# A hybrid diffusion layer stack: the scan begins along the first gate, and scan and attention get smaller shares per weight block

## The chip, the cores and the metric

The kernel runs on one core of one Trainium2 chip. The time is the device time of one execution in microseconds (us). Engines are named as in the profile: PE is TensorE, DVE VectorE, ACT ScalarE, POOL GpSimd, SP SyncE. Each engine works through a queue of its own in a fixed order; an instruction that has to wait holds up everything behind it on its engine.

## The reference

The kernel computes two layers over 256 latent tokens and, in the first layer, 256 context tokens, with 1024 channels. Everything is in float32.

```python
h_l = modulate(rms_norm(x, norm_mix[layer]), mod_l[0], mod_l[1])
# token mixer: three branches on the same input
ssd_l  = ssd_output(y_lf, y_lb, xs_l, h_lat @ w_z, ...)         # two-way state-space scan, 16 heads of 64
na_l   = na_latent(h @ w_q, h @ w_k, h @ w_v, k_c, v_c, rpb) @ na_out   # softmax attention, 8 heads of 64
conf_l = conformer_branch(h @ w_glu, ...)                       # gated, 31-tap convolution per channel
out    = merge_branches(h @ w_gate, (ssd_l, na_l, conf_l)) @ w_o  # sum of sigmoid(gate_b) * branch_b
x = x + mod_l[2] * out
# feed-forward: SwiGLU in layer 0, the best two of eight SwiGLU experts in layer 1
x = x + mod_l[5] * f(modulate(rms_norm(x, norm_ffn[layer]), mod_l[3], mod_l[4]))
```

The scan takes `u`, a five-tap convolution of `h @ w_xbc`, in chunks of 128 tokens: states per chunk (`stS`), a diagonal part per chunk (`ydS`, a 128 x 128 matrix of decays times `C·B`, applied to the inputs), and a part from the carried state.

## The kernel before

All weight products are made in three matmuls of halves: a weight block of 128 x 1024 comes by DMA, ACT makes its high part `h_` (L114) and DVE the low part `l_` (L115), and PE forms high·high, high·low and low·high (L185 to L187). `wstat` keeps a block of weights still and moves the tokens; 512 output columns at a time, in four PSUM banks (the pool `pacc`), from four weight blocks. The next 512 columns can begin only when the four banks were evacuated; for a gate that is ACT's sigmoid at L643.

Token mixing in a layer is a row of steps, named in `ORDER`: `glu`, `dt`, `qkv`, `xbc` make the inputs of the branches, `g0` to `g2` the three gates, `z` the scan's output gate, `p0` to `p2` multiply the branch 0 (scan), 1 (attention), 2 (convolution) by its output weights. The step `ssd` multiplies nothing: it spawns the scan.

Beside these steps run background jobs, written as generators that emit a piece of work and yield its cost: `attention` (L679 ff.; scores S L705, softmax L709 to L714, scaling of P L693, its transposes PT L696, the copy of PT L698, products with v, `po`, L740), `ssd` (states L866 to L900, diagonal part L963 to L989 with the transposes `cbS` L981 and the mask product `MS` L986), `conformer` (31 taps, L534), and the modulation vectors. After each weight block `pump()` (L148) gives each job a credit, its number in `RATE` for this layer, and lets it emit pieces until the credit is spent. `branch` (`p0` to `p2`) first drains its job: all that is left of it is emitted at once. The credits thus set how far a job is spread along the weight blocks. A scheduler with the priorities of `PR` then puts the instructions of each engine into their fixed order.

Background work has four other PSUM banks (`pwk`). Layer 0 works on 512 tokens, layer 1 on 256, so a weight matmul is 128 x 512 there and 128 x 256 here. The profiled execution has the mixer of layer 0 from about 30 to 700 us, its feed-forward to 1150, the mixer of layer 1 to 1560, routing to 1590, and the experts to the end.

Of the kernel before, what the change touches and what calls it, by code (L numbers as in the profile page):

```python
# [53 lines left out]
class Body:  # L54
# [481 lines left out]
    def mix(self, l):  # L536
# [11 lines left out]
        def glu():  # L548
# [15 lines left out]
            cv = self.chunks(4, nt, f"ccv{l}")  # L564
            jobs[2] = self.spawn(self.conformer(l, cu, cv, nt), self.RATE["conv"][l], "conv")

        def qkv():
# [6 lines left out]
            r[1] = self.pair(4, nt, f"o{l}")  # L574
            jobs[1] = self.spawn(self.attention(l, q, kT, v, nt, r[1]), self.RATE["att"][l], "att")

# [5 lines left out]
        def ssd():  # L582
            jobs[0] = self.spawn(self.ssd(l, nt), self.RATE["ssd"][l], "ssd")

        def z():
            zs = self.chunks(KD, nt, "z" + nm)
            self.wstat(W("z"), KD, D, h, tok, lambda o, ps: nc.scalar.activation(zs[o], ps, AF.Silu), "z" + nm)
            if jobs[0] not in self.bg:
                jobs[0] = self.spawn(iter(()), self.RATE["ssd"][l], "ssd")
            jobs[0][0] = chain(jobs[0][0], self.ssd_norm(l, zs, nt))  # L590
# [10 lines left out]
        steps = dict(dt=lambda: self.dt_path(l), glu=glu, qkv=qkv, xbc=xbc, ssd=ssd, z=z)  # L601
        for s in self.ORDER[l].split():
            if s in steps:
# [5 lines left out]
            if full and s == "p1":  # L609
                jobs[3] = self.spawn(self.adas(0, (1, 2)), self.RATE["ada"][0], "ada")  # L610
            if s == "dt" and self.stop == "dt":
# [20 lines left out]
            self.route_ahead(*self.mc[1, 1])  # L632
        self.out_res(self.units(self.a["w_o"][l], 4), KD, m_, range(tok[0] // 128, NB), "wo" + nm)

    ORDER = ("glu dt qkv xbc g1 ssd p1 g2 p2 z g0 p0", "glu dt qkv xbc g1 ssd p1 g2 z p2 g0 p0")
    RATE = dict(conv=(2.0, 2.5), att=(5.0, 2.5), ssd=(7.0, 10.0), ada=(2.6, 2.2))

    def gate(self, l, br, tok):

# [932 lines left out]
    def run(self):  # L1572
# [3 lines left out]
        with ExitStack() as st:  # L1576
# [3 lines left out]
            for l in range(DEPTH):  # L1580
# [12 lines left out]
                if l == 0:  # L1593
                    with self.prio("norm"):
                        self.h = self.hmod(self.col("nffn"), *self.mc[0, 1], f"f{l}")
                    self.mrow = self.mod_rows(self.mod[0, 2], 2, f"f{l}", streams)
                    jobs = [self.spawn(self.adas(1, range(3)), self.RATE["ada"][1], "ada")]
                    self.ffn(0)
# [120 lines left out]
```

## Time and profile before

| what | value |
|---|---|
| three runs | 2400.76, 2401.92, 2401.93 us; median 2401.92 |
| the profiled execution | 2402.24 us, its span 2400.4 us |
| PE busy | 2284.4 us, 95% of the span |
| DVE busy | 1519.2 us, 63% |
| ACT busy | 1041.5 us, 43% |
| mean granted clock of PE | .984 of full speed |

The span reaches from the first to the last instruction; the time of the execution is 1.84 us longer. Busy shares are means over stages with different limits, so they say which engine to look at, and a table by stretch says where. PE's clock has two levels, 1.2 and 2.4 GHz; the granted clock of a stretch is the mean over it, 1.00 for 2.4 GHz.

### The profile page before, as it was taken

To read this page: it belongs to the slowest core of one execution; us is meant where nothing else is said; L and a number is where in the kernel's file an instruction comes from. 1 tells how busy PE (TensorE), PEld (TensorE's weight loads), DVE (VectorE), ACT (ScalarE), POOL (GpSimd) and SP (SyncE) were. 2 spreads that over 40 slices of the span, in tenths; PEclk is the share of its full clock that TensorE was granted. 3 is DMA by queue.
4 is the path that set the end of the run, shared out by engine and by line. 5 is a ranking of instruction groups with operands and counts; after the bars stand their busy time and mean duration, and the time that the engine had idled before them with its cause. 6 is when DMAs were issued, how large, how long until landed. Compare 5 with 4: busy or idle time off the path is not lost.

```text
span 2400.4 us, 30300 instructions
## 1 busy us (share of the span) xinstructions
PE 2284.4 (95%) x11409; PEld 1668.1 (69%) x11409; DVE 1519.2 (63%) x2389; ACT 1041.5 (43%) x1696; POOL 19.0 (1%) x32
## 2 busy tenths in 40 slices
PE   7999989999999999999999999989999998999997
PEld 3777757777777777788877889865666655656554
DVE  3669977677767775535889866643333545655556
ACT  4335645654233222224436585533332444445444
POOL 0000000000000000000000000000000000000000
PEclk9999999999999999999999999979999999999998
DMA  7222223234534555432422333468888899999995
GB/s 275 84 83 79 89 74 97 79 98 127 168 123 135 163 187 182 153 97 96 130 93 88 106 106 123 132 248 331 325 326 342 325 360 374 359 380 341 352 365 223
DMA packets 106283, 469.33 MB, mean 196 GB/s; under 512 B 11536, under 2 KB 12048, under 8 KB 72336
## 3 DMA queue, kind: packets, MB, share of 16 engines
q1 hardware_dynamic: 105280, 464.69, 53.9%
q10 hardware_dynamic: 848, 2.62, 0.3%
q8 instruction: 91, 1.49, 0.2%
q14 instruction: 64, 0.52, 0.1%
HBM read 466.22 MB, written 1.05 MB: 195 GB/s over the span
## 4 chain that ended last, share of the span: by engine, by line
PE 80%; DVE 9%; DMA 5%; ACT 3%; issue 2%; POOL 0%; SPq 0%; POOLq 0%; DVEq 0%; ACTq 0%
PE er L1470 8%; PE nn L1352 7%; PE e L1470 4%; PE edr L1470 4%; DMA adaw<-in_ada_w_dram 4%; PE ndn L1377 4%; PE wg L185 2%; PE wg L186 2%; PE wg L187 2%; PE ed L1470 2%; DVE adac L351 2%; PE xbcL L185 1%; PE ydS L989 1%; PE xbcL L187 1%; PE xbcL L186 1%
## 5 line engine op out<-in xcount | busy, mean ns | idle before, releaser
L351 DVE SCALAR_TENSOR_TENSOR adac<-adaw,sc,adac 128x512 f32<-128x512 f32 x224 | 160.6, 747 | 57.5 <-DMA adaw<-in_ada_w_dram 57.0
L115 DVE TENSOR_TENSOR l_er<-r_er,h_er 128x1024 fp32r<-128x1024 f32 x132 | 154.7, 1219 | 59.8 <-ACT h_er L114 57.6
L1352 PE MATMUL nn<-r_ngun,xn 128*64 128x512 f32 (+1 forms) x768 | 169.3, 561 | 0.0
L114 ACT ACTIVATE h_er<-r_er 128x1024 fp32r<-128x1024 f32 x132 | 133.4, 1053 | 41.7 <-DMA r_er<-in_moe_gu_dram 28.2
L185 PE MATMUL wg<-hHm,h_wg 128*128 128x512 f32 (+1 forms) x384 | 131.4, 343 | 0.0
L187 PE MATMUL wg<-hHm,l_wg 128*128 128x512 f32 (+1 forms) x384 | 130.6, 343 | 0.0
L186 PE MATMUL wg<-hLm,h_wg 128*128 128x512 f32 (+1 forms) x384 | 130.5, 341 | 0.0
L1470 PE MATMUL er<-h_er,gHp 128*128 128x512 f32 (+1 forms) x288 | 110.7, 389 | 17.7 <-ACT h_er L114 17.7
L1352 PEld LDWEIGHTS nn<-r_ngun,xn 128*64 128x64 f32 x768 | 54.3, 137 | 92.1 <-issue 85.1
L1470 PE MATMUL er<-h_er,gLp 128*128 128x512 f32 (+1 forms) x288 | 108.1, 380 | 0.0
L115 DVE TENSOR_TENSOR l_e<-r_e,h_e 128x1024 fp32r<-128x1024 f32 x44 | 52.3, 1222 | 63.2 <-ACT h_e L114 63.0
L1377 PE MATMUL ndn<-r_ndn,hnn 128*64 128x512 f32 x352 | 87.4, 598 | 0.0
L534 DVE SCALAR_TENSOR_TENSOR ccv<-cu,cols,ccv 128x492 f32<-128x492 f32 (+14 forms) x120 | 85.9, 729 | 1.0
L1357 ACT ACTIVATE ntn<-nn 128x512 f32<-128x512 f32 (+1 forms) x24 | 13.5, 561 | 165.7 <-PE nn L1352 165.7
L1470 PE MATMUL er<-l_er,gHp 128*128 128x512 f32 (+1 forms) x288 | 84.0, 380 | 0.0
L1367 DVE TENSOR_TENSOR hnn<-npn,nsn 128x256 f32<-128x256 f32 (+1 forms) x24 | 9.6, 401 | 117.3 <-ACT nsn L1365 117.3
L1470 PEld LDWEIGHTS er<-h_er,gHp 128*128 128x128 f32 x288 | 55.1, 191 | 40.2 <-ACT h_er L114 28.0
L115 DVE TENSOR_TENSOR l_edr<-r_edr,h_edr 128x1024 fp32r<-128x1024 f32 x66 | 77.5, 1220 | 5.8 <-ACT h_edr L114 4.5
L185 PEld LDWEIGHTS wg<-hHm,h_wg 128*128 128x128 f32 x384 | 73.1, 190 | 9.7 <-issue 2.2
L186 PEld LDWEIGHTS wg<-hLm,h_wg 128*128 128x128 f32 x384 | 73.1, 190 | 9.1 <-issue 2.0
L187 PEld LDWEIGHTS wg<-hHm,l_wg 128*128 128x128 f32 x384 | 72.7, 190 | 9.2 <-issue 1.7
L185 PE MATMUL xbcL<-hHm,h_xbcL 128*128 128x512 f32 (+1 forms) x192 | 74.9, 390 | 0.0
(656 smaller groups left out, 6067.5 us busy)
## 6 DMA issues: line engine op xcount, KB each, us to landing
r_ngun<-in_moe_gu_dram SPq DMA_DIRECT2D x88, 1024.0 KB, 7.1
r_er<-in_moe_gu_dram SPq DMA_DIRECT2D x66, 1024.0 KB, 7.3
r_ndn<-in_moe_down_dram SPq DMA_DIRECT2D x44, 1024.0 KB, 7.3
adaw<-in_ada_w_dram SPq DMA_DIRECT2D x160, 256.0 KB, 3.1
r_edr<-in_moe_down_dram SPq DMA_DIRECT2D x33, 1024.0 KB, 7.6
r_wg<-in_w_in_dram SPq DMA_DIRECT2D x48, 512.0 KB, 3.5
r_e<-in_moe_gu_dram SPq DMA_DIRECT2D x22, 1024.0 KB, 7.3
r_xbcL<-in_w_in_dram SPq DMA_DIRECT2D x24, 512.0 KB, 3.5
```

The costliest lines, as they stand in the source:

```text
L114: nc.scalar.activation(Hd, src, AF.Copy)
L115: nc.vector.tensor_tensor(Ld, src, Hd.bitcast(F32), op=ALU.subtract)
L185: mm(out, wh, xh, start=(first and kk == 0), stop=False, skip_group_check=True)
L186: mm(out, wh, xl, start=False, stop=False, skip_group_check=True)
L187: mm(out, wl, xh, start=False, stop=(kk == kc - 1), skip_group_check=True)
L351: nc.vector.scalar_tensor_tensor(d, w, c, d, op0=ALU.mult, op1=ALU.add)
L534: nc.vector.scalar_tensor_tensor(y[:, :, a:b], x[:, :, a + s:b + s], w[:, k:k + 1], y[:, :, a:b], op0=ALU.mult, op1=ALU.add)
L989: nc.tensor.matmul(pd[64 * (i % 2):64 * (i % 2) + 64, (hl // 2) * 128:(hl // 2 + 1) * 128], xd[r][:, hl * 64:(hl + 1) * 64], M[:, i, :], s ...
L1352: mm(ps[64 * h:64 * h + 64, :n], x[kk], w[:, h, k, :], start=(kk == 0), stop=(kk == KD - 1), skip_group_check=True)
L1357: nc.scalar.activation(t, ps[:, :n], AF.Copy)
L1377: mm(ps[64 * h:64 * h + 64], hT[:, kk * 64:(kk + 1) * 64], w[:, h, k, :], start=(kk == 0), stop=(kk == fc - 1), skip_group_check=True)
L1470: mm(ps[s][j], st[kk], w[p][:, k, :], start=(kk == 0 and p == 0 and q == 0), stop=(kk == kc - 1 and p == 1), skip_group_check=True)
```

## The change

In layer 0 and in layer 1 the scan is spawned before the first gate instead of behind it, so that it gets credit at the eight weight blocks of that gate too. The credits per weight block, for (layer 0, layer 1): attention from (5.0, 2.5) to (3.6, 2.8), the scan from (7.0, 10.0) to (3.8, 3.4). The rest stays.

```diff
--- before.py
+++ after.py
@@ -632,8 +632,8 @@
             self.route_ahead(*self.mc[1, 1])
         self.out_res(self.units(self.a["w_o"][l], 4), KD, m_, range(tok[0] // 128, NB), "wo" + nm)
 
-    ORDER = ("glu dt qkv xbc g1 ssd p1 g2 p2 z g0 p0", "glu dt qkv xbc g1 ssd p1 g2 z p2 g0 p0")
-    RATE = dict(conv=(2.0, 2.5), att=(5.0, 2.5), ssd=(7.0, 10.0), ada=(2.6, 2.2))
+    ORDER = ("glu dt qkv xbc ssd g1 p1 g2 p2 z g0 p0", "glu dt qkv xbc ssd g1 p1 g2 z p2 g0 p0")
+    RATE = dict(conv=(2.0, 2.5), att=(3.6, 2.8), ssd=(3.8, 3.4), ada=(2.6, 2.2))
 
     def gate(self, l, br, tok):
 
```

What the order of the engines becomes is seen at three places. First PE in layer 0, where the scan's diagonal part begins, in the kernel before: `cbS` are the transposes of the decay sums, `ydS` the matmuls that need the mask product made from them on ACT and DVE.

```order
L963 MATMUL scS_2621<-uL_10_1134,uL_8_1133 128x128 x2
L866 MATMUL xtyS_2627<-con_t,uL_0_1129 128x128 x2
L866 MATMUL xtyS_2627<-con_t,uL_2_1130 128x128 x2
L981 MATMUL cbS_2637<-con_t,cs_669 128x128 x4
L989 MATMUL ydS_2636<-MS_2642,xdS_2632 64x128
L981 MATMUL cbS_2653<-con_t,cs_669 128x128
```

The changed kernel, the same place of the scan; `wg` are weight matmuls of gate 2 (29 of them stand there in all, of which these are the first):

```order
L963 MATMUL scS_2366<-uL_10_1134,uL_8_1133 128x128 x2
L866 MATMUL xtyS_2372<-con_t,uL_0_1129 128x128 x2
L866 MATMUL xtyS_2372<-con_t,uL_2_1130 128x128 x2
L981 MATMUL cbS_2382<-con_t,cs_669 128x128 x4
L187 MATMUL wg_0_2467<-hHm_254,l_wg_0_2474 128x512
L185 MATMUL wg_0_2467<-hHm_254,h_wg_0_2473 128x512
L186 MATMUL wg_0_2467<-hLm_256,h_wg_0_2473 128x512
```

Before, `ydS` stands right behind `cbS`; now it comes after the 29 weight matmuls.

Second, PE in layer 1 at the last two head pairs of attention, in the kernel before (`PT` transposes of softmax rows, `S` scores, `wg` gate 1, first chunk):

```order
L696 MATMUL PT_10161<-con_t,P_10144 128x128 x4
L696 MATMUL PT_10198<-con_t,P_10145 128x128
L705 MATMUL S_10206<-kTL_2_8962,qL_0_8960 128x512
L696 MATMUL PT_10198<-con_t,P_10145 128x128
L705 MATMUL S_10207<-kTL_2_8962,qL_0_8960 128x512
L696 MATMUL PT_10198<-con_t,P_10145 128x128 x2
L187 MATMUL wg_1_10346<-hHm_8478,l_wg_2_10412 128x256
L185 MATMUL wg_2_10347<-hHm_8478,h_wg_2_10411 128x256
```

The changed kernel: the last weight matmul of the first chunk of gate 1, then the same work.

```order
L187 MATMUL wg_3_10348<-hHm_8478,l_wg_3_10523 128x256
L696 MATMUL PT_10127<-con_t,P_10110 128x128 x4
L696 MATMUL PT_10168<-con_t,P_10111 128x128
L705 MATMUL S_10176<-kTL_2_8962,qL_0_8960 128x512
L696 MATMUL PT_10168<-con_t,P_10111 128x128
L705 MATMUL S_10177<-kTL_2_8962,qL_0_8960 128x512
L696 MATMUL PT_10168<-con_t,P_10111 128x128 x2
L696 MATMUL PT_10197<-con_t,P_10180 128x128 x4
L696 MATMUL PT_10234<-con_t,P_10181 128x128 x4
L740 MATMUL po_10240<-PT_10101,vL_0_8963 64x256
L881 MATMUL btS_10384<-con_t,uL_8_9463 128x128 x2
L866 MATMUL xtsS_10389<-con_t,uL_0_9459 128x128 x2
```

Before, weight matmuls stood between the scores and the transposes of the last pair. Now none does; weight matmuls begin again, with the second chunk of gate 1, after 16 `PT`, the value matmuls and eight `stS`.

Third, ACT in layer 1 around the evacuation of that first chunk (`g` from `wg`, L643), in the kernel before:

```order
L643 ACT_TABLE_LOAD
L643 ACTIVATE g_0_10343<-wg_0_10345 128x256
L643 ACTIVATE g_0_10343<-wg_1_10346 128x256
L114 ACTIVATE h_wg_1_10509<-r_wg_1_10507 128x1024
L643 ACTIVATE g_0_10343<-wg_2_10347 128x256
L643 ACTIVATE g_0_10343<-wg_3_10348 128x256
L713 ACT_TABLE_LOAD
L713 ACTIVATE P_10210,st_10137<-S_10206,st_10137 128x256
```

The changed kernel (`hsS1c` and `s0S` are copies of the scan's states from `stS`):

```order
L698 COPY PT_10102<-PT_10234 128x4x128
L883 ACTIVATE BpS_10387<-btS_10384 128x256
L897 ACTIVATE hsS1c_10379<-stS_10396 128x512
L897 ACTIVATE s0S_10383<-stS_10401 128x512
L114 ACTIVATE o1H_0_9457<-po_10240 128x256
L897 ACTIVATE hsS1c_10379<-stS_10411 128x512
L897 ACTIVATE s0S_10383<-stS_10416 128x512
L883 ACTIVATE BpS_10422<-btS_10419 128x256
L897 ACTIVATE hsS1c_10380<-stS_10467 128x512
L643 ACT_TABLE_LOAD
L643 ACTIVATE g_0_10343<-wg_0_10345 128x256
L643 ACTIVATE g_0_10343<-wg_1_10346 128x256
```

Before, the evacuation stood ahead of the exponentials (L713, L714) of the last head pair; now it stands behind them, behind the last copy of `PT` and behind five copies of states.

## Rows read from the trace of the kernel before

**Rows 1.** The page's head and the first row of its engine table: busy time, share of the span, instructions.

```profile
span 2400.4 us, 30300 instructions
...
PE 2284.4 (95%) x11409; PEld 1668.1 (69%) x11409; DVE 1519.2 (63%) x2389; ACT 1041.5 (43%) x1696; POOL 19.0 (1%) x32
```

**Rows 2.** Engine time by stretch of 60 us: the stretch, its length, then the busy time (and instructions) of PE, of PE's weight loads, DVE, ACT and POOL, the granted clock of PE as a share of full speed, the share of the DMA engines and GB/s.

```profile
300.00:360.00 60.00, 51.14 (x227) 32.80 (x226) 47.27 (x87) 26.70 (x55) 0.00 (x0) 0.97 0.23 74
420.00:480.00 60.00, 55.74 (x305) 42.27 (x306) 40.18 (x65) 39.23 (x77) 0.00 (x0) 0.94 0.25 79
1320.00:1380.00 60.00, 59.98 (x408) 49.15 (x408) 50.33 (x88) 34.28 (x62) 0.00 (x0) 1.00 0.32 106
```

**Rows 3.** The list of PE's waits, 300 to 360 us: who waited, for what, the sum in us, how many waits, and the longest.

```profile
PE PT L696 <- DVE P L693: 1.8, 2, 1.5
PE stS L890 <- DVE xeS L888: 1.7, 2, 1.6
PE po L740 <- DVE PT L698: 0.8, 1, 0.8
```

**Rows 4.** Engine time by stretch of 4 us, with the columns of rows 2.

```profile
356.00:360.00 4.00, 4.00 (x18) 2.98 (x17) 3.12 (x5) 2.69 (x9) 0.00 (x0) 0.67 0.47 135
...
424.00:428.00 4.00, 3.74 (x21) 3.41 (x22) 2.62 (x5) 3.98 (x6) 0.00 (x0) 0.50 0.05 17
428.00:432.00 4.00, 4.00 (x14) 3.21 (x14) 0.00 (x0) 3.99 (x14) 0.00 (x0) 0.71 0.00 0
```

**Rows 5.** The timeline of layer 0, PE and last one row of DVE: start, time in us, engine, line, instruction, how many in a run, and in brackets the idle time before it and its releaser.

```profile
321.19 0.39 PE L185 MATMUL wb0na_out<-o0H,h_wb0na_out 128*128 128x512 f32 x1
...
324.13 0.39 PE L186 MATMUL wb0na_out<-o0L,h_wb0na_out 128*128 128x512 f32 x1
...
331.28 1.09 PE L696 MATMUL PT<-con_t,P 128*128 128x128 f32 x8 [1.48 <-DVE P L693]
...
335.56 1.98 PE L890 MATMUL stS<-xeS,BpS 128*128 128x512 f32 x4
...
354.62 0.43 PE L989 MATMUL ydS<-MS,xdS 128*64 128x128 f32 x2 [4.49 <-DVE MS L986]
...
424.26 1.12 PE L989 MATMUL ydS<-MS,xdS 128*64 128x128 f32 x8 [4.69 <-DVE MS L986]
...
330.25 0.88 DVE L693 TENSOR_SCALAR P<-P,st 128x512 f32<-128x512 f32 x2
```

**Rows 6.** Groups of instructions by line and shape, layer 0's mixer (60 to 700 us), DVE and last two rows of ACT: how many, busy us and mean ns of one, then the idle time before them and what ended it.

```profile
L115 DVE TENSOR_TENSOR l_wg<-r_wg,h_wg 128x1024 fp32r<-128x1024 f32 x24 | 29.3, 1223 | 11.8 <-ACT h_wg L114 11.4 <-PE wb0na_out L187 0.3
...
L693 DVE TENSOR_SCALAR P<-P,st 128x512 f32<-128x512 f32 x16 | 7.0, 481 | 0.0
L709 DVE TENSOR_TENSOR P<-S,bt 128x256 f32<-128x256 f32 x16 | 6.7, 421 | 2.9 <-PE S L705 2.7
L711 DVE TENSOR_REDUCE st<-P 128x1 f32<-128x256 f32 x16 | 6.6, 410 | 0.0
...
L534 DVE SCALAR_TENSOR_TENSOR ccv<-cu,cols,ccv 128x498 f32<-128x498 f32 x8 | 5.9, 733 | 0.1
...
L714 ACT ACTIVATE P<-P,st 128x256 f32<-128x256 f32 x16 | 8.1, 504 | 0.0
...
L713 ACT ACTIVATE P<-S,st 128x256 f32<-128x256 f32 x16 | 7.5, 470 | 8.0 <-DVE st L712 8.0
```

**Rows 7.** The same view of DVE, 1300 to 1400 us (layer 1): the five-tap convolution in front of the scan; the 31-tap one of layer 0 uses the same lines.

```profile
L534 DVE SCALAR_TENSOR_TENSOR cvL<-uL,cols,cvL 128x508 f32<-128x508 f32 x8 | 5.9, 742 | 0.0
...
L534 DVE SCALAR_TENSOR_TENSOR cvL<-uL,cols,cvL 128x255 f32<-128x255 f32 x4 | 1.8, 478 | 0.0
L531 DVE TENSOR_SCALAR cvL<-uL,cols 128x256 f32<-128x256 f32 x2 | 0.8, 404 | 0.0
```

**Rows 8.** Engine time by stretch of 10 us, with the columns of rows 2.

```profile
310.00:320.00 10.00, 9.97 (x42) 6.71 (x41) 8.74 (x21) 5.29 (x12) 0.00 (x0) 1.00 0.16 52
320.00:330.00 10.00, 9.80 (x42) 7.43 (x40) 5.41 (x9) 9.02 (x15) 0.00 (x0) 1.00 0.18 54
...
1310.00:1320.00 10.00, 10.00 (x57) 6.43 (x56) 8.84 (x19) 5.47 (x11) 0.00 (x0) 1.00 0.27 80
1320.00:1330.00 10.00, 10.00 (x70) 8.19 (x70) 9.99 (x21) 6.92 (x13) 0.00 (x0) 1.00 0.41 128
1330.00:1340.00 10.00, 10.00 (x85) 9.95 (x84) 8.99 (x19) 9.09 (x19) 0.00 (x0) 1.00 0.40 137
```

**Rows 9.** The timeline of layer 1 around the last softmax group but one and the first evacuation of gate 1: a row of DVE, one of PE, two of ACT.

```profile
1325.31 0.88 DVE L693 TENSOR_SCALAR P<-P,st 128x512 f32<-128x512 f32 x2
...
1325.94 0.73 PE L696 MATMUL PT<-con_t,P 128*128 128x128 f32 x5
...
1331.95 1.28 ACT L643 ACT_TABLE_LOAD   x1
1333.24 0.66 ACT L643 ACTIVATE g<-wg 128x256 f32<-128x256 f32 x2
```

**Rows 10.** The timeline of PE in the routing stage, and engine time by stretch of 4 us behind it.

```profile
1569.68 0.45 PE L1414 MATMUL ohp<-con_t,oh 128*128 128x128 f32 x1 [5.24 <-issue]
...
1580.00:1584.00 4.00, 4.00 (x20) 4.00 (x20) 0.58 (x2) 1.12 (x5) 0.00 (x0) 0.50 0.48 203
1584.00:1588.00 4.00, 4.00 (x22) 3.77 (x22) 1.27 (x6) 1.99 (x5) 0.00 (x0) 0.57 0.00 0
```

## The prediction

> **What bounds the kernel now.** I read the page first: its engine table has TensorE (PE) busy for 2284.4 of a span of 2400.4 us [rows 1], so only what makes PE wait, or takes its clock away, costs time. The profiled execution took 2402.24 us, 1.84 beyond its span and 0.32 above the median of 2401.92; the sum below is made against 2402.24. Then I read tables of engine time by stretch for the places where the diff works. In layer 0 PE is idle 60 − 51.14 = 8.9 us of 300 to 360 us and 60 − 55.74 = 4.3 us of 420 to 480 us; in layer 1 it is busy 59.98 of 60 us around the same work [rows 2]. The list of PE's waits names them: transposes of softmax rows (PT) behind VectorE's (DVE's) scaling of P, the scan's state matmuls (stS) behind xeS, the value matmuls (po) behind the copy of PT [rows 3], and two waits of 4.49 and 4.69 us of the scan's diagonal product (ydS) behind DVE's MS [rows 5]. Last I read the granted clock around them: .67 in 356–360 us, .50 in 424–428 and .71 in 428–432 [rows 4]. Clock lost there: .33 × 4 + .50 × 3.74 + .29 × 4 = 4.4 us of PE work not done. So layer 0 holds 13.1 + 4.4 = 17.5 us that could be won, and layer 1 nothing.
>
> **The change, layer 0.** Attention and scan get less credit at each weight block, so attention lasts longer. The weight matmuls that stand on PE ahead of the last PT transposes fall from 996 to 864: 132 fewer. One starts 2.94 / 13 = .226 us after another (321.19 to 324.13, fourteen of them [rows 5]), so PE arrives 29.8 us sooner: 331.28 − 1.48 = 329.80 becomes 300.0. DVE has ahead of the same scaling 20 convolution taps (.73) and 5 weight splits (1.22) fewer [rows 6, 7], 14.6 + 6.1 = 20.7 us, and was idle for 1.26 + 4.59 us in the 20 us before [rows 8]. The scaling ended at 330.25 + .88 = 331.13; without that work it ends at 310.4, and if all the idle time is closed too, at 304.6. PE therefore waits 4.6 to 10.4 us if no more changes; I take 5.0, nearer the low end, because DVE's idle time there is waiting for weight splits that now come earlier. Behind it four taps (2.9 us) now stand on DVE between the scaling and the PT copy, where none stood and where DVE had 1.28 us free between the two; PE's wait for that copy grows from .8 to .8 + 2.9 − 1.3 = 2.4. The stS waits were 1.7 in sum [rows 3]; four weight matmuls (.226 each) that stood between them are gone: 2.6.
>
> What goes are the ydS waits. Between the mask matmuls cbS and the ydS that needs their result there now stand 29 weight matmuls, 6.6 us of work against 4.49 waited; the second bare pair is covered in the same way. That cover holds as long as the blocks' weights are there; without it 9.2 us come back.
>
> The clock: a wait of 5 us at about 300 us can cost as little as the 1.3 us after 352 or as much as the 3.1 after 424 [rows 4]; I take 2.2. For the rest of layer 0, between 0 and the present 4.4, I take 1.5. Sum: 5.0 + 2.4 + 2.6 + 2.2 + 1.5 = 13.7 against 17.5, a gain of 3.8 us.
>
> **The change, layer 1.** Here the scan starts before gate 1 and attention's share is larger than before (2.8 for 2.5). Before, the last two head pairs' transposes and scores stood between weight matmuls, and ScalarE (ACT) evacuated the first column chunk of gate 1 between two groups of softmax exponentials. Now that evacuation, which frees the four accumulators for chunk 1, stands on ACT behind five copies of scan states. PE's in-order row between the two chunks holds no weight matmul: PT, two S, PT, po, bt, xts, po, four stS and their transposes run bare, each behind a short DVE or ACT step. PE comes to the first PT after 37 more weight matmuls than it did at 1325.94 [rows 9], .118 each (85 in 10 us [rows 8]): 1330.3. DVE comes to its scaling after 2 full taps (.74), 8 half taps (.48), one first tap (.40) [rows 7] and 3 splits (1.22) more: 9.4 us, from 1325.31 + .88 = 1326.2 to 1335.6; its idle time of 1310–1330, 10 − 8.84 + .01 = 1.2 us [rows 8], brings that to 1334.4 at the earliest. So PE waits 4.1 to 5.3: 4.7.
>
> Then the bare chain from scores to the next scaled P: three DVE steps (.42 + .41 + .41) and a negation (.2), the exponentials .47 + .50 with two accumulator reads (.19 each), sum and reciprocal (.16 + .17), scaling .48 [rows 6] (the short ones are estimates, from the one-column steps that stand beside them in the timeline), 3.6 us, less the .25 of transposes PE has in the meantime and some overlap of the two heads: 3.2. The copy ahead of po: .6, near layer 0's .8 [rows 3]. The state steps between stS and stS, four bare ones against the stS waits of layer 0 [rows 3]: 2.1. The clock, with 10.6 us of waiting in one place: at least the 1.3 of 352–360 [rows 4]; at most half speed for a stretch such as the one after 1569.68, where a wait of 5.24 us was followed by .50 until past 1584 [rows 10], 9 us; I take 3.5, near the 3.1 that the 4.69 us wait cost. Sum: 4.7 + 3.2 + .6 + 2.1 + 3.5 = 14.1 us lost where nothing was lost.
>
> The table load of that evacuation is 1.28 us, and the activation behind it starts at once (1331.95, then 1333.24 [rows 9]); before, it ran while PE had weight matmuls; now chunk 1 waits for it, which I count inside the 2.1. The Trainium skill, page "ScalarE: Activation LUTs", section "What ACT_TABLE_LOAD costs", has 1.28 us for the load, as the trace does, but adds 1.38 of drain, 2.66 for a switch. No row here shows the drain; by the page the sum would be 1.4 higher.
>
> The order of the dense feed-forward and of the experts is the same in both kernels, so I count nothing there. Net: 14.1 − 3.8 = +10.3, so 2412.5 profiled, 2412 at the median.
>
> **The rivals.**
> *A, the clock stays down in layer 1.* After 1569.68 the clock stayed at .50, which is the lower of its levels (1.2 of 2.4 GHz), for some 15 us [rows 10]. The bare block holds 16 records of stS at 1.98 / 4 and 42 transposes at 1.09 / 8 [rows 5], 13.6 us, and with its scores and value matmuls, for which I add 3.5 as an estimate, some 17 us of PE work; if PE goes through it at half speed, what isn't hidden in the waits is about 8 us more: 2420, at most 2428. For it: several waits stand close together. Against it: PT, po and stS waits of .8 to 1.6 us between 331 and 348 [rows 3] are followed by .90 and .67 only after the 4.49 us wait [rows 4, 5]. The Trainium skill, page "TensorE: Matmul & The Clock Gate", section "HAM oscillation — how this bites in real kernels", says that bursts of matmuls with waits between them each begin at the low clock. The stretch after 1569.68 agrees with it, the one from 331 to 348 doesn't. Its chance is .17.
> *B, no change.* The long PT wait of layer 1 doesn't come, because DVE reaches the scaling in time, and with it the clock's loss: 14.1 − 4.7 − 3.5 = 5.9 us lost against a gain in layer 0 of about 6 (the 3.8, and the clock's 2.2 if the PT wait is short there too): 2402. For it: the scheduler's order ranks DVE's scaling above the taps, and a few taps more or less decide. Against it: the 9.4 us are counted from the order. Its chance is .17.
> *C, faster.* DVE reaches the scaling before PE in both layers. The mechanism is DVE's idle time in layer 0: 5.85 us of it stood just ahead of the scaling [rows 8], and there may be more to close further back. From the point at which 10 us close, the PT wait (5.0) and its clock (2.2) are gone, and the gain of layer 0 becomes 11; layer 1 loses only its bare chain, 5.9: 2397. For it: 9.2 us of ydS waits surely go. Against it: it needs both. Its chance is .15.
>
> **How the numbers follow.** The forecast has .51; its own range, with its terms at their ends, is 2406 to 2419. A change within .2% (4.8 us, about what a measurement of this kernel tells from none) is 2397.1 to 2406.7. Rival C falls just on the fast side of that: faster .15. B and a little of the forecast's low end: same .19. The forecast's rest and A: slower .66. The range that leaves out no more than 2 in 10 reaches from 2399 (B with its terms at the low end) to 2423 (A without its far end).
>
> **What would show it.** Right: no ydS wait above 1 us in layer 0; a PT wait of about 5 us near 300 us and one near 1330; between two gate chunks of layer 1 a stretch of some 25 us with no weight matmul and PE busy for little more than half of it; granted clock below .8 there; the same times from 1590 us to the end, shifted. Wrong, if layer 1 shows no wait above 2 us (then B or C), if the clock stays at .50 for over 10 us (A), or if the feed-forward and expert stages change their length, which I priced at nothing.

## The result and the profile after

The changed kernel takes 2428.19 us (median of four runs, 2422.09 to 2430.51) against 2401.34 for the kernel before (2400.69 to 2401.93): a ratio of 1.0103, 95% interval 1.009 to 1.0115. By the medians it is 27 us slower, by the ratio 25; 10 were forecast, and the range ended at 2423. The profiled execution took 2427.2 us, 25.0 more than the one before.

The page after, its head and the first row of its engine table, which answer to [rows 1]:

```profile
span 2425.3 us, 30291 instructions
...
PE 2292.9 (95%) x11409; PEld 1670.7 (69%) x11409; DVE 1516.9 (63%) x2389; ACT 1040.8 (43%) x1695; POOL 19.4 (1%) x32
```

PE makes the same 11409 matmuls. Its busy time grew by 8.5 us, because matmuls at the lower clock take longer, and the rest of the 24.9 us of span, 16.4 us, is waiting. Where, the first and last matmuls of each stage tell (from the lists of instructions by tile; the differences are those of the unrounded times):

| stage, from its first matmul to the next stage's | before | after | difference |
|---|---|---|---|
| layer 0 mixer (`ggL` to `fg`) | 30.0 to 730.1 | 30.0 to 734.0 | +3.9 |
| feed-forward (`fg` to the last `fd`) | to 1134.2 | to 1134.9 | -3.1 |
| start of layer 1 (to its first `xbcL`) | to 1229.1 | to 1231.2 | +1.4 |
| layer 1 mixer (to its first `woL`) | to 1526.3 | to 1549.3 | +20.8 |
| routing (to the first `nn`) | to 1590.0 | to 1613.0 | 0.0 |
| experts, to the last matmul | to 2384.6 | to 2409.5 | +1.9 |

The three stages that the change doesn't touch (feed-forward, start of layer 1, experts) move by -3.1, +1.4 and +1.9. In the fifteen kernels below they move by -5.5 to +2.8, 0 to +1.5 and -1.0 to +3.3, so no more is made of them here. What counts is +3.9 in layer 0 and +20.8 in layer 1.

Each of the two mixers as one stretch, with the columns of [rows 2], layer 0 and layer 1 before, then layer 0 and layer 1 after:

```profile
30.00:730.10 700.10, 679.69 (x3270) 503.65 (x3271) 520.48 (x877) 320.17 (x598) 4.58 (x5) 0.99 0.32 103
1229.10:1526.30 297.20, 295.66 (x2047) 250.32 (x2046) 220.54 (x399) 183.64 (x344) 2.11 (x5) 1.00 0.35 111
...
30.00:734.00 704.00, 679.56 (x3271) 503.54 (x3272) 518.93 (x877) 316.47 (x595) 5.07 (x5) 0.99 0.30 102
1231.20:1549.30 318.10, 301.99 (x2047) 252.22 (x2047) 220.27 (x399) 187.06 (x346) 1.95 (x5) 0.98 0.30 103
```

In layer 0 PE is idle for 24.4 us instead of 20.4, and busy as long as before. In layer 1 it is idle for 16.1 us instead of 1.5, and busy 6.3 us longer for the same matmuls, at a lower granted clock.

Engine time by stretch, the three stretches of [rows 2]:

```profile
300.00:360.00 60.00, 52.08 (x274) 36.71 (x274) 55.37 (x91) 32.64 (x71) 0.00 (x0) 0.91 0.28 92
420.00:480.00 60.00, 59.97 (x347) 45.81 (x346) 43.40 (x70) 36.65 (x74) 0.00 (x0) 1.00 0.26 88
1320.00:1380.00 60.00, 48.97 (x280) 35.23 (x280) 42.38 (x80) 23.94 (x49) 0.00 (x0) 0.89 0.20 67
```

The second stretch is mended, the first has nearly as much waiting as before (7.9 us for 8.9) and less clock (.91 for .97), and the third, which was full, lost 11 us of PE time and a tenth of its clock.

The waits of PE in the changed kernel, from its timeline, six rows of layer 0 and then four of layer 1:

```profile
304.32 1.94 PE L696 MATMUL PT<-con_t,P 128*128 128x128 f32 x8 [5.24 <-DVE P L693]
307.41 1.11 PE L740 MATMUL po<-PT,vL 128*64 128x256 f32 x2 [1.15 <-DVE PT L698]
...
323.23 1.12 PE L890 MATMUL stS<-xeS,BpS 128*128 128x512 f32 x2 [1.58 <-DVE xeS L888]
...
410.10 0.32 PE L797 MATMUL rbln<-con_t,rrln 128*128 128x128 f32 x1 [1.70 <-POOL rrln L794]
...
520.20 0.50 PE L187 MATMUL zL<-hHm,l_zL 128*128 128x512 f32 x1 [3.42 <-DVE l_zL L115]
...
590.21 0.32 PE L797 MATMUL rbyS<-con_t,rryS 128*128 128x128 f32 x1 [1.21 <-POOL rryS L794]
...
1337.82 1.30 PE L696 MATMUL PT<-con_t,P 128*128 128x128 f32 x5 [5.71 <-DVE P L693]
1347.73 1.94 PE L696 MATMUL PT<-con_t,P 128*128 128x128 f32 x8 [3.58 <-DVE P L693]
1359.34 1.95 PE L890 MATMUL stS<-xeS,BpS 128*128 128x512 f32 x4 [0.88 <-DVE xeS L888]
1362.52 0.70 PE L890 MATMUL stS<-xeS,BpS 128*128 128x512 f32 x1 [0.79 <-DVE xeS L888]
```

The two waits of 4.49 and 4.69 us for `MS` [rows 5] are gone. In layer 1 the two PT waits alone are 9.3 us. The granted clock around them, in stretches of 4 us:

```profile
1332.00:1336.00 4.00, 0.11 (x1) 0.00 (x0) 3.56 (x10) 3.89 (x8) 0.00 (x0) 1.00 0.68 219
1336.00:1340.00 4.00, 2.18 (x6) 1.43 (x7) 1.91 (x5) 0.75 (x4) 0.00 (x0) 0.62 0.27 109
1340.00:1344.00 4.00, 4.00 (x7) 0.97 (x5) 1.51 (x5) 0.00 (x0) 0.00 (x0) 0.50 0.00 0
1344.00:1348.00 4.00, 0.42 (x3) 0.30 (x3) 2.20 (x8) 2.48 (x9) 0.00 (x0) 0.50 0.00 0
1348.00:1352.00 4.00, 4.00 (x22) 2.60 (x22) 1.13 (x2) 0.97 (x2) 0.00 (x0) 0.67 0.02 4
```

Clock lost, as in the prediction, busy time by what is missing of the clock: .38 × 2.18 + .50 × 4.00 + .50 × .42 + .33 × 4.00 = 4.4 us. The last rows of this kernel are ACT's, where the first chunk of gate 1 is evacuated:

```profile
1361.33 0.60 ACT L897 ACTIVATE hsS1c<-stS 128x512 f32<-128x512 f32 x1 [2.61 <-PE stS L890]
1361.94 1.28 ACT L643 ACT_TABLE_LOAD   x1
1363.24 1.21 ACT L643 ACTIVATE g<-wg 128x256 f32<-128x256 f32 x4
```

PE had ended that chunk at 1332.1; its banks were free at 1364.4, 32 us later.

### The profile page after: what moved, and what is told of

Read it like the earlier page. It is cut to its first block, busy times and chain, and to the rows that moved or that the text cites. A ratio compares the mean times of both kernels' runs of the same rounds, so it can differ in the third digit from the quotient of the medians.

```text
span 2425.3 us, 30291 instructions
## 1 busy us (share of the span) xinstructions
PE 2292.9 (95%) x11409; PEld 1670.7 (69%) x11409; DVE 1516.9 (63%) x2389; ACT 1040.8 (43%) x1695; POOL 19.4 (1%) x32
## 4 chain that ended last, share of the span: by engine, by line
PE 72%; issue 11%; DVE 8%; DMA 4%; ACT 3%; POOL 0%; SPq 0%; POOLq 0%; DVEq 0%; ACTq 0%
PE er L1470 7%; PE nn L1352 7%; PE e L1470 4%; PE edr L1470 4%; PE ndn L1377 4%; DMA adaw<-in_ada_w_dram 3%; PE ed L1470 2%; PE wg L185 2%; PE wg L186 2%; PE wg L187 2%; DVE adac L351 2%; PE fd L234 1%; PE fd L233 1%; PE fd L232 1%; PE ada L356 1%
## 5 line engine op out<-in xcount | busy, mean ns | idle before, releaser
L114 ACT ACTIVATE h_wg<-r_wg 128x1024 fp32r<-128x1024 f32 x48 | 50.6, 1057 | 62.6 <-PE wg L186 33.5
```

The costliest lines, as they stand in the source:

```text
L114: nc.scalar.activation(Hd, src, AF.Copy)
```

## The experiments

All ratios are to the kernel before, run in turn on the same chip. The two columns at the right are the change of the layer 0 and layer 1 mixers in the profiled execution, between the same matmuls as in the table above. Layer 0 mixers of the same code lie up to 4 us apart (+4.7, +2.6 and +2.4 of the changed code; -6.3, -6.0, -2.6 and -3.2 of the new shares with the old spawn place), layer 1 mixers of the same code within 1.

| run | what differs from before | ratio (95%) | layer 0 | layer 1 |
|---|---|---|---|---|
| changed kernel | both layers: spawn and shares | 1.0103 (1.009 to 1.0115) | +3.9 | +20.8 |
| e1 | both: spawn | 1.0268 (1.0247 to 1.029) | +53.6 | +14.2 |
| e2 | both: shares | 1.0119 (1.0091 to 1.0148) | -6.3 | +31.7 |
| e3 | layer 0: spawn and shares | 1.0002 (.9992 to 1.0012) | +4.7 | 0.0 |
| e4 | changed kernel, attention 2.5 in layer 1 | 1.0063 (1.0044 to 1.0082) | +2.6 | +15.6 |
| e5 | changed kernel, half banks | 1.0053 (1.0039 to 1.0068) | +4.4 | +13.8 |
| e6 | layer 0: shares | .9974 (.9964 to .9984) | -6.0 | 0.0 |
| e7 | layer 1: scan's share 3.4 | 1.0082 (1.0067 to 1.0096) | +1.0 | +18.6 |
| e8 | layer 1: attention's share 2.8 | 1.0112 (1.0096 to 1.0128) | +1.4 | +29.0 |
| e9 | as e5, one start flag per bank | 1.0054 (1.0037 to 1.007) | +2.4 | +13.8 |
| e10 | changed kernel, four `adaw` buffers | 1.0089 (1.0071 to 1.0106) | +3.6 | +21.2 |
| e11 | layer 0: attention's share 3.6 | .9977 (.9967 to .9986) | +0.8 | 0.0 |
| e12 | as e6, four `adaw` buffers | .9969 (.9958 to .9981) | -3.8 | 0.0 |
| e13 | layer 0 as e6; layer 1: spawn, half banks | 1.0007 (.9992 to 1.0021) | -2.6 | +8.3 |
| e14 | as e13, scan's share 3.4 in layer 1 | .9993 (.9979 to 1.0007) | -3.2 | +7.6 |
| e15 | layer 1: half banks alone | 1.008 (1.0064 to 1.0097) | -1.0 | +19.1 |

**The two parts of the change, and its two layers (e1 to e4).** Theory T puts the layer 1 loss on attention's larger share, rival R on the early spawn.

e1:
```diff
-    ORDER = ("glu dt qkv xbc g1 ssd p1 g2 p2 z g0 p0", "glu dt qkv xbc g1 ssd p1 g2 z p2 g0 p0")
+    ORDER = ("glu dt qkv xbc ssd g1 p1 g2 p2 z g0 p0", "glu dt qkv xbc ssd g1 p1 g2 z p2 g0 p0")
```


> Both layers spawn the scan before the first gate, all shares as before. Theory T: what costs most in layer 1 is attention's larger share (2.8 for 2.5), because the last two softmax groups then stand behind the whole first chunk of gate 1 (waits of 5.7 and 3.6 us and 4.6 us of clock in the changed kernel). With the old share weight matmuls stand between those groups again, so layer 1 loses only its bare scan states, 2 to 5 us, and the kernel takes 2401 to 2410. Rival R: the early spawn costs most, because the evacuation of the first gate chunk stands on ACT behind the scan's copies whatever the share; with 10 credits even more scan work stands there, so layer 1 loses 15 us or more and the kernel takes 2416 or more.

e2:
```diff
-    RATE = dict(conv=(2.0, 2.5), att=(5.0, 2.5), ssd=(7.0, 10.0), ada=(2.6, 2.2))
+    RATE = dict(conv=(2.0, 2.5), att=(3.6, 2.8), ssd=(3.8, 3.4), ada=(2.6, 2.2))
```


> The new shares alone, the scan spawned behind the first gate as before. Theory T: the last two softmax groups of layer 1 still run with no weight matmul between them, so a wait of 3 to 4 us for the scaled P and some clock stay, and the time is 2406 to 2418. Rival R: without the early spawn layer 1 is as before, 2398 to 2405.

e3 (layer 0 of both lines, layer 1 as before):
```diff
+    ORDER = ("glu dt qkv xbc ssd g1 p1 g2 p2 z g0 p0", "glu dt qkv xbc g1 ssd p1 g2 z p2 g0 p0")
+    RATE = dict(conv=(2.0, 2.5), att=(3.6, 2.5), ssd=(3.8, 10.0), ada=(2.6, 2.2))
```


> Layer 0 changed in full, layer 1 as before. By the account of the two traces (mixer of layer 0 +4.2, its feed-forward -3.1, the start of layer 1 +1.4 of clock) 2401 to 2406 under both theories. If it is 2410 or more, layer 0 sets back more than its own stretch shows; if it is under 2399, the layer 0 half is a gain.

e4 (against the changed kernel):
```diff
-    RATE = dict(conv=(2.0, 2.5), att=(3.6, 2.8), ssd=(3.8, 3.4), ada=(2.6, 2.2))
+    RATE = dict(conv=(2.0, 2.5), att=(3.6, 2.5), ssd=(3.8, 3.4), ada=(2.6, 2.2))
```


> The changed kernel with one number back: attention's share in layer 1 is 2.5 instead of 2.8. Theory T: both waits for the scaled P and the clock go, 13.9 us, so 2412 to 2416; the stS waits stay. Rival R: the early spawn decides, so 2424 to 2430.

Both theories missed, R by less. e1's layer 1 lost 14.2, just short of R's 15 and far from T's 2 to 5; its total of 64 us is layer 0's, which neither had considered. e2 lost more in layer 1 than the whole change does. e4 gave 5.2 us of layer 1 back, where T expected 13.9 and R nothing. Layer 1 of e1, e4 and the changed kernel takes the three parts in one after another: the spawn costs 14.2 us, the scan's share 1.4 more, attention's share 5.2 more. Only e3 came as expected: by its ratio the layer 0 half of the change costs nothing that can be told from noise, while its profiled mixer is 4.7 us longer. So that layer 0 got slower rests on the profiles; the ratio shows that the 3.8 us forecast as its gain are not there. What the 5.2 are, the list of PE's waits of e4 in layer 1 shows (who waited for what; sum, number, longest):

```profile
PE PT L696 <- DVE P L693: 4.5, 2, 4.1
PE stS L890 <- DVE xeS L888: 1.7, 2, 0.9
...
PE po L740 <- DVE PT L698: 0.8, 1, 0.8
```

One of the two PT waits is left, 4.1 us, with the same 1.7 of `stS`. With 2.5 one group of transposes is covered by weight matmuls again; the last one still comes after the end of the chunk. e1's layer 0, as one stretch and in its longest waits:

```profile
28.50:782.30 753.80, 700.97 (x3271) 515.76 (x3272) 521.72 (x877) 314.84 (x594) 3.70 (x5) 0.94 0.30 96
...
PE PT L696 <- DVE P L693: 16.0, 5, 5.5
PE ada L356 <- DVE adac L351: 10.1, 3, 8.6
PE ydS L989 <- DVE MS L986: 9.9, 4, 4.8
PE wg L185 <- ACT g L643: 5.3, 2, 4.6
```

Of the 53.6 us, 32 are idle time (52.8 for 20.4) and 21 are longer busy time at a granted clock of .94 for .99. The early scan at 7.0 makes a longer bare stretch, from 290 to 343 us without a weight matmul, and later steps are late too. The last row is PE waiting for the evacuation of a gate by ACT.

**The banks (e5, e9, e13 to e15).** Theory B: weight matmuls of the second chunk cannot stand in the bare stretch, because the first chunk holds all four banks until it is evacuated. In layer 1 a sum has 256 columns of a bank's 512, so two sums can share one bank and leave two banks for the next chunk. The diff does this in all three gates of layer 1.

e5 (against the changed kernel):
```diff
-            ps = [self.acc(f"{name}{c}_{o}") for o in range(n // 128)]
+            if name.startswith("wg1") and n == 512:
+                pp = [self.acc(f"{name}{c}_{o}") for o in range(2)]
+                ps = [pp[o // 2][:, (o % 2) * 256:(o % 2) * 256 + 256] for o in range(4)]
+            else:
+                ps = [self.acc(f"{name}{c}_{o}") for o in range(n // 128)]
```


> The changed kernel, but each 512-column chunk of a gate in layer 1 uses half of two PSUM banks instead of one half of each of four (256 tokens fill half a bank), so the second chunk need not wait until the first is evacuated. Theory B: the stretch without weight matmuls comes from the banks that the first chunk holds until ACT evacuates it behind the scan's copies. PE then has 25 weight matmuls more ahead of the first late PT and 22 between the two (.118 each), so the waits of 5.7 and 3.6 us become about 2.7 and 1.0, the stS waits go and most of the 4.6 us of clock; the layer 1 mixer is 8 to 11 us slower than before instead of 20.8, and the kernel about 11 us faster than the changed one (ratio to before 1.004 to 1.007). Rival R: the scan's pieces stand ahead of the second chunk because they were emitted earlier and have the higher priority, and the banks play no part: nothing changes, ratio 1.009 to 1.012.

In e5 both sums of a bank begin with the start flag, and the kernel's output is off by a relative error of .08; in e9 only the first sum does, and the values are the reference's:
```diff
-                mm(out, wh, xh, start=(first and kk == 0), stop=False, skip_group_check=True)
+                mm(out, wh, xh, start=(first and kk == 0 and not (o % 2 and name.startswith("wg1"))), stop=False, skip_group_check=True)
```


> The same instructions in the same order as in the kernel with the half banks, but of the two sums that share a bank only the first one begins with the start flag. Theory B: the time is that of the half banks again, ratio to before 1.004 to 1.007. If the flag has a part in the time, it is outside of that.

Both came in at the expected ratio, .005 under the changed kernel. e9's waits of PE in layer 1:

```profile
PE wg L187 <- DVE l_wg L115: 2.9, 6, 0.6
PE wg L185 <- ACT h_wg L114: 2.3, 2, 1.3
PE ydS L993 <- DVE MS L990: 1.9, 2, 1.6
PE stS L894 <- DVE xeS L892: 0.9, 3, 0.5
```

None of the 9.3 us of PT waits is left, and half of the `stS` waits. Weight matmuls stand between the transposes, as three rows of e9's timeline show, and below them its layer 1 mixer as one stretch:

```profile
1344.02 0.44 PE L700 MATMUL PT<-con_t,P 128*128 128x128 f32 x2
1344.21 0.48 PE L187 MATMUL wg<-hHm,l_wg 128*128 128x256 f32 x2
...
1349.61 1.91 PE L700 MATMUL PT<-con_t,P 128*128 128x128 f32 x8
...
1232.80:1543.80 311.00, 302.18 (x2047) 254.92 (x2046) 220.29 (x399) 184.86 (x344) 1.95 (x5) 0.98 0.32 106
```

Only the banks and the start flag were changed in the program, so the held banks had kept the weight matmuls out. R's ground, that the scan's pieces merely rank first, falls. But the mixer got only 7.0 us shorter, not 10 to 13: PE now comes to the next weight blocks before ACT and DVE have split them (the first two rows of waits, 5.2 us). And PE's busy time is that of the changed kernel, 302 us: idle time was won back, the clock was not.

e13 and e14 ask what the rest belongs to; both have e6's layer 0 (below) and e9's banks. e13, against e9:
```diff
-    ORDER = ("glu dt qkv xbc ssd g1 p1 g2 p2 z g0 p0", "glu dt qkv xbc ssd g1 p1 g2 z p2 g0 p0")
-    RATE = dict(conv=(2.0, 2.5), att=(3.6, 2.8), ssd=(3.8, 3.4), ada=(2.6, 2.2))
+    ORDER = ("glu dt qkv xbc g1 ssd p1 g2 p2 z g0 p0", "glu dt qkv xbc ssd g1 p1 g2 z p2 g0 p0")
+    RATE = dict(conv=(2.0, 2.5), att=(3.6, 2.5), ssd=(3.8, 10.0), ada=(2.6, 2.2))
```


> Layer 0 with the new shares and the old spawn place (6.0 us gained before); layer 1 with the early spawn, half banks and the old shares (2.5, 10.0). Theory B: with the banks out of the way and the old shares the early spawn costs little: of the 14.2 us that it cost the PT wait of 4.1, po .8, most of the stS waits (4.2) and 3.0 of clock go, so the layer 1 mixer is 1 to 4 us longer than before and the kernel 2 to 5 us faster than before (ratio .998 to .9995). Rival S: the spawn puts work on DVE ahead of the weight splits whatever the banks do; layer 1 then keeps 8 us or more, and the kernel is slower than before.

e14, against e13: `ssd=(3.8, 10.0)` becomes `ssd=(3.8, 3.4)`.

> As the run before, with the scan's share in layer 1 at 3.4 for 10.0. If the scan's share makes the rest of layer 1 (it cost 18.6 us with the late spawn), this one is 8 us or more slower than the run before. If the rest is attention's 2.8, the two are equal within 3 us.

Layer 1 is +8.3 and +7.6, so with the early spawn the scan's share plays next to no part (nor did it between e1 and e4), and e9's 13.8 holds some 6 us of attention's share, as e4 had 5.2. The 8.3 is what rival S had for layer 1; that the kernel is slower than before, as S also had it, its ratio doesn't show. e15 is the control: the kernel before with the two diffs of e5 and e9, and nothing of the change.

> The kernel before with the half banks for the layer 1 gates, nothing else. If the rest of 8.3 us is the early spawn's, this kernel's layer 1 mixer is within 1.5 us of before and the ratio is .999 to 1.001. If the half banks cost it, by weight matmuls that run ahead of their blocks' splits, layer 1 is 4 to 8 us longer here too and the ratio is 1.001 to 1.0035.

It missed by far: +19.1 us in layer 1, where before there was next to no wait.

```profile
PE rcyS L789 <- ACT ysqS L944: 4.1, 1, 4.1
PE stS L894 <- DVE xeS L892: 1.7, 2, 0.9
...
PE zL L185 <- ACT h_zL L114: 1.3, 1, 1.3
```

The half banks thus have a cost of their own, in a schedule that did not need them, and the 8.3 us can't be put down to the spawn alone. That share stays open.

**The shares in layer 1 with the late spawn (e7, e8).** Diffs against before: `ssd=(7.0, 10.0)` to `(7.0, 3.4)`; and `att=(5.0, 2.5)` to `(5.0, 2.8)`.

> Only the scan's share in layer 1 is changed, 3.4 for 10.0, spawned behind the gate as before. With both layer 1 shares new the layer 1 mixer was 31.7 us longer, and of its waits the ydS, rowa and zL ones (about 11 us) and their clock stand late in the mixer. If they belong to the scan's share, this kernel is 14 to 20 us slower than before; if attention's share makes them too, under 8.

> Only attention's share in layer 1 is changed, 2.8 for 2.5. Of the 31.7 us the two PT waits (5.7) and the clock of 13.7 us at half speed around them should be its part: 10 to 14 us slower than before. If the scan's share makes them, no change.

e7 is as expected, e8 twice as dear: 29.0 us. Its waits in layer 1:

```profile
PE PT L696 <- DVE P L693: 5.7, 2, 3.6
PE rcyS L785 <- ACT ysqS L940: 3.5, 1, 3.5
PE stS L890 <- DVE xeS L888: 2.0, 2, 1.8
```

The PT waits are the ones expected; the scan's norm (`rcyS`) at the end of the mixer came on top, and a second stretch at half clock behind it:

```profile
1508.00:1524.00 16.00, 14.97 (x53) 11.77 (x54) 6.61 (x19) 6.22 (x15) 0.82 (x4) 0.50 0.00 0
```

Alone, the shares cost 18.6 and 29.0, together 31.7 (e2): such costs don't add.

**Layer 0 (e6, e10 to e12).** e6, against before: `att=(5.0, 2.5)` to `(3.6, 2.5)`, `ssd=(7.0, 10.0)` to `(3.8, 10.0)`.

> Only the layer 0 shares are changed (attention 3.6, scan 3.8); spawn places and layer 1 as before. In the kernel with all new shares and the old spawn places the layer 0 mixer took 6.3 us less than before. If that is the shares' own doing, this kernel is 5 to 7 us faster than before (ratio .997 to .998). If it came with something of layer 1, there is no change.

It is 6 us faster, as expected, and faster than both kernels. e11 has attention's part of it alone, `att=(3.6, 2.5)`:

> Only attention's share in layer 0 is changed, 3.6 for 5.0. The two layer 0 shares together gave 6.0 us. If attention's share carries it, because the last PT no longer stands between bare pieces, this kernel is 4 to 7 us faster than before; if the scan's share carries it, because the two ydS waits of 4.5 and 4.7 us belong to its 7.0, this kernel is within 2 us of before.

Its ratio says 5.5 us, as if attention's share carried nearly all; its profiled layer 0 is not shorter (+0.8) and its feed-forward 3.2 shorter, a stage that moves by itself. The split of the gain between the two shares stays open.

The wait of 3.42 us at `zL` has this on DVE, in the changed kernel:

```profile
514.50 1.41 DVE L351 SCALAR_TENSOR_TENSOR adac<-adaw,sc,adac 128x512 f32<-128x512 f32 x2 [1.56 <-DMA adaw<-in_ada_w_dram]
517.59 1.41 DVE L351 SCALAR_TENSOR_TENSOR adac<-adaw,sc,adac 128x512 f32<-128x512 f32 x2 [1.68 <-DMA adaw<-in_ada_w_dram]
518.92 1.22 DVE L115 TENSOR_TENSOR l_zL<-r_zL,h_zL 128x1024 fp32r<-128x1024 f32 x1
```

The split that PE needs stands behind background work that waits for a load. e10 gives that load more buffers:
```diff
-                w = self.stg.tile([128, 512], F32, name=f"adaw{l}{g}{j}{k}", tag="araw", bufs=2)
+                w = self.stg.tile([128, 512], F32, name=f"adaw{l}{g}{j}{k}", tag="araw", bufs=4)
```
(and the same at its other use).

> The changed kernel with four buffers instead of two for the modulation weights (adaw) that DVE waits for in layer 0. Theory Q: PE's wait of 3.4 us at the weight block of z comes because DVE has two adac steps queued ahead of the split, and these wait for their DMA; with loads further ahead that wait and its clock (1.7 us) go, and some of the later ada wait (0.6): layer 0's mixer 4 to 6 us shorter than in the changed kernel, ratio to before about 1.008 to 1.009. Rival: the split is late because ACT and DVE are behind on other work; then layer 0 keeps the wait and the time is that of the changed kernel, 1.009 to 1.0115.

The wait at `zL` is gone, and the ratio lies in Q's range, though its interval reaches well into the rival's. But the layer 0 mixer isn't shorter (+3.6 for +3.9), because the end of the modulation work now makes PE wait:

```profile
PE ada L356 <- DVE adac L351: 4.5, 1, 4.5
```

Q had the place and the cause of the wait right, but the gain in the mixer was given back 85 us later. The ratio is .0014 (3 us) under the changed kernel's, with intervals that overlap; whether that is a gain, and from where, isn't shown. e12 has e6 and the buffers:

> The kernel with only the layer 0 shares changed, and four buffers for the modulation weights. Its layer 0 has a wait of 3.4 us for adac near the end of the mixer (at 621 us); if loads further ahead remove it, the kernel is 8 to 11 us faster than before (ratio .9955 to .9967); if not, 6 us as without the buffers (.9974).

It has the lowest ratio of all, .9969, but its interval holds e6's .9974, and in the profile the waits at the end of the mixer stay; that the buffers help is not shown. What beats both kernels is e6's line: old places of spawn, new shares in layer 0 alone.

## Why the prediction was wrong

The forecast was +10.3 us on the profiled execution and +25.0 were measured. Of the 14.7 missed, 7.7 are layer 0's (forecast -3.8, measured +3.9) and 6.7 layer 1's (14.1, 20.8).

- **What bounds the kernel, and where.** Right: PE's waits and clock, at the places named.
- **Layer 0, the terms that were worked out.** PT 5.24 (5.0 forecast), `po` 1.15 (2.4), `stS` 2.46 (2.6), and no `ydS` wait. The four taps ahead of the copy of PT cost less, because at the lower clock PE took 1.94 us for its transposes, not 1.09.
- **Layer 0, the step that failed:** "For the rest of layer 0, between 0 and the present 4.4, I take 1.5." It counted clock alone, and only the two places of before. New waits came at places whose queues the prediction had not followed: 1.77 at the first weight matmul of gate 1 (272 us), 1.70 `rbln`, 3.42 `zL`, 1.00 `rcyS`, 1.21 `rbyS` (.76 before), .58 `ada`, 9 us in sum with the .76 off; and the clock: 3.8 us around 304 (forecast 2.2), 1.7 at 272 and 1.7 at 520. These terms are 7.5 us more than the 17.5 of before (8.85 + 8.9 + 7.2), not 3.9. The idle time alone gives 4.0 (24.4 for 20.4), and PE's busy time didn't grow, so the clock lost here was made up elsewhere in the mixer; where isn't shown.
- **Layer 1, the terms that were worked out.** PT 5.7 (4.7), the bare chain 3.6 (3.2), `po` nothing (.6), `stS` 1.7 (2.1), clock 4.4 (3.5): 15.4 against 14.1. The place and the mechanism held, and the sizes nearly, the PT wait's with some luck: PE came to it at 1332.1 (1330.3 worked out) and was released at 1337.8 (1334.4 to 1335.6), both some 2 us late.
- **Layer 1, the step that failed:** the sum ended where the second chunk of gate 1 begins, and later work was taken to be as before. Of the other 5.4 of 20.8, eight waits of .3 to .9 us between 1380 and 1520 (`ydS`, weight splits, evacuations) make 4.4, where before had one of .4; the rest isn't assigned.
- **The cause that was given,** the evacuation behind the scan's copies, held in part: e9 shows that the four held banks keep the weight matmuls out. But sparing them gave back 7.0 of the 20.8 us, and half banks have a cost of their own (e15), so how much of the loss the banks make isn't settled. Attention's share, named in half a sentence, was a second cause of 5 to 6 us (e4, e9 against e14).
- **The rivals.** A had a time near the result, but not its reason: the clock came back at 1351 and cost 4.4 us, .9 more than the forecast, not 8. The routing stage, from which A took its stretch at half clock, was misread: the clock was at half speed there before the wait of 5.24 us began at 1564.4, so that wait isn't what brought it down.

```profile
1560.00:1564.00 4.00, 1.46 (x9) 1.39 (x8) 3.01 (x13) 0.21 (x1) 0.56 (x1) 0.51 0.00 0
```

The rule of the Trainium skill, page "TensorE: Matmul & The Clock Gate", section "HAM oscillation — how this bites in real kernels", on which A leaned, is told there of bursts of matmuls behind waits on DMA of some 3 to 5 us. The trace agrees for such waits: the bursts at 1337.82 and 1347.73, behind waits of 5.71 and 3.58 us, began at the low clock. Those at 1359 and 1362, behind .88 and .79, did not, and neither they nor the short waits from 331 to 348 that the prediction held against the rule are its case.

B and C fell: DVE reached neither scaling before PE. The table load took 1.28 us and the activation began at once (1361.94, then 1363.24). The Trainium skill, page "ScalarE: Activation LUTs", section "What ACT_TABLE_LOAD costs", adds a drain to the load; as before the change, the trace doesn't show one.

- **The range.** Its upper end, 2423, was rival A without its far end. Neither it nor the forecast's own upper end, 2419, had a term for the queues that weren't followed.

## What to carry to other kernels

A background job's start and its share act together: the early spawn cost 54 us in the layer 0 mixer with the old shares and 5 to 11 with the new ones, and the new shares with the old spawn place gained 3 to 6 us in layer 0 and lost 32 in layer 1. Change them one at a time and one layer at a time; here the half of the change that helped was hidden by the rest. Where a fixed order moves, walk every in-order queue from the first moved row to where the two orders agree again, not only the rows of the waits that go: some 13 us of waiting came from places where next to nothing had waited before. And where PE runs bare, ask which banks it would need for the work that could cover it, and who frees them.

## What the runs showed of the hardware

In the kernel before, a wait of 4.49 us was followed by some 3 us of half clock and one of 4.69 us by some 6 [rows 4, 5]; in the changed kernel, behind the 5.24 us wait, the clock was .50 over two stretches of 4 us, though PE was full in the second:

```profile
304.00:308.00 4.00, 2.53 (x10) 1.85 (x10) 4.00 (x7) 0.59 (x1) 0.00 (x0) 0.50 0.18 74
308.00:312.00 4.00, 4.00 (x17) 2.08 (x16) 2.71 (x5) 0.38 (x1) 0.00 (x0) 0.50 0.00 0
```

The clock fell behind short waits too. In e9 no wait near 1337 us was longer than 1.08, but there were three between 1333 and 1338.3 (.61, 1.08, .51), and the clock fell:

```profile
1336.00:1340.00 4.00, 2.44 (x12) 2.23 (x13) 2.44 (x5) 2.42 (x7) 0.00 (x0) 0.81 0.37 103
1340.00:1344.00 4.00, 4.00 (x13) 2.03 (x11) 1.77 (x4) 0.00 (x0) 0.00 (x0) 0.76 0.24 95
```

Waits of .8 to 1.6 us spread over 331 to 348 us had not done so in the kernel before [rows 3, 5].
